# Seven row loads beside the output projection, a weights' place opened inside a stage, and a mixture four steps sooner

## The chip, the cores and the metric

The kernel runs on one core of a Trainium2 chip. A core has five engines with instruction queues of their own: PE (matrix products), DVE (vector work), ACT (scalar functions), POOL (GpSimd) and SP, which here only issues transfers. POOL issues transfers too. Each engine takes its instructions in order and waits on semaphores for the others. Sixteen DMA engines carry all transfers of the core.

The metric is the time of one execution on the device, in microseconds. The kernel before takes 2197.03 us (median of three runs, 2195.69 to 2200.31).

## The reference

One layer of a bidirectional encoder, run on two sets of tokens with the same weights: a long set of 1024 tokens (`A` in the code, the prompt) and a short one of 512 (`B`, the sample), 1024 features each.

```python
h = rms_norm(x, pre_w)
cols = jnp.einsum('bsd,dc->bsc', h, w_in)          # one input projection
m_qk, m_v, m_o, m_z, m_i, m_f, a_qkv, a_z, gate = jnp.split(cols, ...)
y_m = mlstm_mixer(m_qk, m_v, m_o, ...) * silu(m_z)  # branch m: 4 heads x 256, both directions
y_a = dilated_attention(a_qkv, rel_table) * silu(a_z)  # branch a: 3 dilations x 8 heads x 64
p_m, p_a = y_m @ w_pm, y_a @ w_pa
g = sigmoid(gate)                                   # two gates per channel
merged = g[0] * p_m + g[1] * p_a
out = merged @ w_out
return x + rms_norm(out, post_w)
```

The dilated attention computes three groups (dilations 1, 4, 16), each with its own softmax over a window and a bias taken from a table, and then mixes the three outputs per token and head by their softmax maxima and denominators. That mixing is called the mixture here.

## The kernel before

All matrix products are done in two parts of each operand, a high and a low one, as three matmuls (`mm3`, L232): high x high, high x low, low x high. One `mm3` with 512 columns is called a step.

**Order of the work.** The input projection of the long set comes first. Then PE runs one recurrence or attention after the other, and between their pieces it runs steps of a second stream, the `Fill` (L137): the input projection of the short set, then the two branch projections and the output projection of the long set (`outputs`, L2249), then those of the short set (`branches`, L2542, and `final`, L2613). `fill(share)` runs as many steps as the stage's rate says. For PE and SP the program's order is the order on the engine; for DVE, ACT and POOL a planner orders the instructions by a model of their times.

The stretch that matters begins at step 768 of the fill (`SHORT`), where only the last four of the short set's input units are left, which make gates (8 steps each):

- the short set's attention, `N.attend(B, ...)` (L2940), 48 tiles in rounds. In each round PE does one tile's logits (`lg`, two buffers), later its transposes (`pt`) and products (`o`), and 6.25 steps of the fill (4.75 in the last third). DVE adds the bias from a table that SP loads from `erow` and takes the maximum (L1867, L1758), ACT the exponential. Outputs go to `og_b` in memory.
- beside it, in the fill: the four gate units with `begin` alongside (L2315, one of its yields per step), which loads quadrants of the long set's rows and splits the first; then 112 steps of the first branch projection, 64 of the second, and the long set's output projection (L2445), 112 steps counted by `n` (L2528). The latter's finished rows are added to `y_prompt` in memory by accumulating transfers on POOL, held in the list `adds`.
- after the attention, the short set's mixture, `N.combine(B, ...)` (L2950). It loads `og_b` for 128 tokens at a time (L2131, L2138), computes weights (`weigh`, L2078), scales the three parts (`mix`, L2097), adds them (`add`, L2104), and PE transposes the sum (`turn`, L2108, line L2111). Each of its pieces goes to DVE only behind the last eviction issued so far (`self.evicted`). Between its pieces the fill runs `STEPS[4]` = 30 steps in four shares and then `STEPS[5]` = 46 steps in 14.
- the rest of the fill: the short set's projections.

**Buffers and queues that the change touches.**

- Weights are held in places of one high and one low tile (`N.wsplit`). Three exist from the start. Where the short set's gates had their own store buffers (`N.sw`, four of 512 columns), a fourth place is opened at L2931 to L2933, at step 768: the stores still pending from these buffers are issued on SP, and the memory is then taken as a place. A store reads what an ACT instruction (L1059) wrote.
- The last four gates are stored from the residual buffers `xo` (`N.late`, L2939, four in rotation). The same buffers later hold rows of the input for the residual sum of the short set (L2669 to L2672).
- The eight rows of the short set's branch m (`ym_b`, 128 x 512 each) are split into high and low parts by `split_rows` (L2218): ACT L2224, DVE L2225. It goes along with the output projection from n = 86. Rows 0 to 3 go to the places H2 and X0, rows 4 to 7 to K0 and Q1, which hold operands of the output projection until its last quarter. Rows 0, 1 and 2 are loaded at n = 44, 50 and 56 (L2519) into three buffers (`rows_in`: `sraw` and two `ymr`), rows 3 to 7 after the attention (L2943 to L2945) into five more (`ymx`). All eight loads are SP's.
- In the short set's first branch projection (L2555) the transfers left in `adds` go out at every second step (L2566).

Of the kernel before, what the change touches and what calls it, by code (L numbers as in the profile page):

```python
# [22 lines left out]
F32 = mybir.dt.float32  # L23
# [6 lines left out]
P = 128  # L30
D = 1024
KT = D // P
BLK = 512
# [173 lines left out]
class Net:  # L207
# [2002 lines left out]
                    self.fetch(("ym", T.S, min(r // 2, 4)), t[:, :w], T.ym[r, :, b * BLK:b * BLK + w])  # L2210
                yield

    def row_load(self, T, tiles, k):

        t = tiles[k]
        self.fetch(("ym", T.S, k // 2), t, T.ym[k])

# [31 lines left out]
    def outputs(self, T, before):  # L2249
# [20 lines left out]
        def slots(name):  # L2270
            x = four(name, F32R)
            return [(x[:, 0], x[:, 1]), (x[:, 2], x[:, 3])]
# [42 lines left out]
        def begin():  # L2315
            for name, at in (("a0", "K0"), ("b0", "K1"), ("a1", "X0"), ("b1", "Q1")):
                M[name] = four(at)
            for n, (name, row, b) in enumerate((("a0", 0, 0), ("b0", 4, 0))):
                quadrant(name, row, b)
                for _ in range((6, 18)[n]):  # L2320
                    yield
            M["even"] = slots("V0b") + slots("V1b")
            for k in range(4):
                divide(made, ("m", 0, k), M["even"][k], M["a0"][:, k])
                yield
# [119 lines left out]
        def final(weights):  # L2445
# [3 lines left out]
            n = 0  # L2449
            tiles = [(i, t) for i in range(7) for t in range(4)]  # L2450
# [55 lines left out]
            w, p = {}, {}  # L2506
            for s in range(len(tiles) + 1):
                for z in (s - 1, s):
                    if not 0 <= z < len(tiles):
                        continue  # L2510
                    (i, t), kp = tiles[z], s - z
                    if t == 0:
                        w[kp] = [y.rearrange("p (k c) -> p k c", c=S) for y in weights(i == kp == 0)]
                    if kp == 0:
                        p[z] = self.dense()
                    for k in (2 * kp, 2 * kp + 1):
                        give(jobs, n)
                        give(self.adds, n)
                        if n in (44, 50, 56):  # L2519
                            self.row_load(*self.after, (n - 44) // 6)  # L2520
                        hi, lo = made["f", i, k]
                        c = slice(t * P, (t + 1) * P)
                        self.mm3(p[z], (hi[:, c], lo[:, c]), (w[kp][0][:, k % 2], w[kp][1][:, k % 2]), k == 0, k == 3)
                        if k == 3:
                            evict(i, t, p.pop(z))
                        if t == 3 and k % 2:
                            weights.__self__.release()
                        n += 1  # L2528
                        yield
# [12 lines left out]
    def branches(self, T, b, odd, before):  # L2542
# [12 lines left out]
        def proj_m(weights):  # L2555
            m2[:] = [self.place(1 - odd, i, F32) for i in (0, 2)]
            fill = weights.__self__
            gate(1, 0)
            for ct in range(KT):
                wm = weights()  # L2560
                pm = self.dense()
                if ct == 4:
                    assert not self.adds
                    self.more_places(fill, [[z[:, 1024 * i:1024 * (i + 1)] for i in range(2)] for z in map(self.take, ("H0", "H3"))])
                for k in range(KT):
                    if k % 2 and self.adds:  # L2566
                        self.adds.pop(0)[1]()
                    c = slice(k * P, (k + 1) * P)
                    hi, lo = yb[k // 4]
                    self.mm3(pm, (wm[0][:, c], wm[1][:, c]), (hi[:, k % 4], lo[:, k % 4]), k == 0, k == KT - 1)  # L2570
                    if k == 3:
                        gate(*((1, ct + 1) if ct < KT - 1 else (0, 0)))
                    if k == KT - 1:
                        self.evicted = nc.vector.scalar_tensor_tensor(m2[ct // 4][:, ct % 4], gates.pop((1, ct)), 1.0, pm, op0=OP.add, op1=OP.mult)
                    yield
# [103 lines left out]


SHORT = 768
STEPS = (316, 260, 192, (6.25, 4.75), 30, 46)
QUADS = (0, 1, 5, 6, 3, 4, 7)
PRE_A, PRE = 28, 32

# [1 line left out]
def body(tc, a):  # L2687
    N = Net(tc, a)
    nc = tc.nc
    (x1, y1), (x2, y2) = a["runs"]  # L2690
    with ExitStack() as st:
# [13 lines left out]
        with ExitStack() as s1:  # L2705
# [4 lines left out]
            with ExitStack() as sv:  # L2710
# [34 lines left out]
                for i in range(2):  # L2745
                    p = ps.tile([P, BLK], F32, name="d")
# [114 lines left out]
        with ExitStack() as s1:  # L2861
# [13 lines left out]
            fill = Fill(N, units)  # L2875
# [7 lines left out]
            with ExitStack() as s2, tc.issue_after(N.splits[0].ins), tc.issue_after(N.splits[1].ins):  # L2883
                end = N.short_input(N.pool(s2, "turn", 6, "right", PSUM), xt)
# [12 lines left out]
            with ExitStack() as s2:  # L2897
# [30 lines left out]
                        pass  # L2928
                    N.flush(lambda p: True)
                fill.until(SHORT)  # L2930
            N.flush(lambda p: p[3] is not None and p[3][0] is N.sw)  # L2931
            sw = sw_tile()
            N.wsplit.insert(0, [sw[:, 1024 * i:1024 * (i + 1)] for i in range(2)])  # L2933
            fill.ahead, N.side = 4, nc.gpsimd
            N.osb = N.pool(s1, "out", 1, "left")
            N.rows_in = [N.sraw[:, :BLK]] + [N.osb.tile([P, BLK], F32, name=f"ymr{i}") for i in range(2)]
# [3 lines left out]
            N.attend(B, fill, STEPS[3], kept["qkv"], ("lg", "o", "pt"), 7)  # L2940
            end = N.pool(s1, "end", 1, "right")
            N.ps_d.append(N.pool(s1, "ps_e", 2, "left", PSUM))
            N.after[1][3:] = [end.tile([P, BLK], F32, name=f"ymx{i}") for i in range(5)]  # L2943
            for k in range(3, KT):
                N.row_load(*N.after, k)  # L2945
            N.xo_bufs.insert(0, ("late", [end.tile([P, BLK], F32, name=f"xo2{i}") for i in range(2)]))
            with ExitStack() as s2:
                cmb_ps = N.pool(s2, "cmb_ps", 2, "right", PSUM)
# [80 lines left out]
```

## Time and profile before

| | |
|---|---|
| median of three runs | 2197.03 us |
| lowest, highest | 2195.69, 2200.31 us |
| profiled execution | 2199.68 us |
| its span, first to last instruction | 2197.9 us |
| mean granted clock of TensorE | 0.995 |
| DMA, mean over the span | 213 GB/s |

The profile is of one execution. A group's row gives line, engine, operation, tiles and count. A row of the timeline begins with start and duration in us; in brackets stands how long the engine was idle before it and what released it. A row of the waits is: who waited, for whom, total us, times, longest. A row of the windows is: the stretch, its length, then the busy us and instructions of PE, PEld (weight loads), DVE, ACT and POOL, the granted clock (1.00 is full), the mean busy share of the DMA engines, and GB/s. A row of the transfers is: transfer, issuing queue, count, size, median us from issue to landing.

### The profile page before, as it was taken

Reading aid. Unit: us, or ns where it says so; the run is one execution under the profiler, and the core shown is the slowest. Engines: PE = TensorE matmul, PEld = TensorE weight load, DVE = VectorE, ACT = ScalarE, POOL = GpSimd, SP = SyncE. Lnnn points to the kernel's source line nnn. Section 1 sums busy time; section 2 is a strip of 40 time slices with the busy share of each in tenths; the row PEclk is TensorE's granted clock in tenths of the full one; section 3 lists DMA queues with packets and bytes.
Section 4 is the critical chain, followed back from the end, with each engine's and each line's share of the span. In section 5 each row is a group of like instructions: output and inputs, shape, how many; then the busy total and the mean of one; then the engine's idle time right before and its main releaser. Section 6 shows DMA issues by size and latency. Waiting matters only on the chain.

```text
span 2197.9 us, 33826 instructions
## 1 busy us (share of the span) xinstructions
PE 2164.9 (98%) x11530; PEld 1841.9 (84%) x11530; DVE 1543.4 (70%) x3011; ACT 1084.2 (49%) x2248; POOL 800.9 (36%) x1053
## 2 busy tenths in 40 slices
PE   9999999999999999999999999999999999999798
PEld 8988888888777888888888889998788878888686
DVE  8766676768887987547888775574668837675773
ACT  7322344444444444446777666666755534435321
POOL 1000444333233875325776650011045522331531
PEclk9999999999999999999999999999999999999999
DMA  5642687955456554367646558886668778876972
GB/s 214 190 140 71 209 274 248 302 201 198 164 184 218 201 201 157 134 204 266 194 164 231 169 168 265 240 240 194 199 234 276 248 250 306 289 238 224 256 280 96
DMA packets 233944, 469.05 MB, mean 213 GB/s; under 512 B 38282, under 2 KB 120394, under 8 KB 233643
## 3 DMA queue, kind: packets, MB, share of 16 engines
q1 hardware_dynamic: 199304, 343.00, 48.0%
q0 software_dynamic: 30864, 111.29, 15.8%
q10 hardware_dynamic: 3602, 12.59, 1.4%
q8 instruction: 91, 1.49, 0.3%
q14 instruction: 83, 0.67, 0.1%
HBM read 314.56 MB, written 156.43 MB: 214 GB/s over the span
## 4 chain that ended last, share of the span: by engine, by line
PE 59%; DMA 4%; issue 3%; DVE 2%; POOL 1%; ACT 1%; SPq 0%; DVEq 0%; POOLq 0%; ACTq 0%
PE dense L235 11%; PE dense L236 11%; PE dense L237 11%; PE d L237 4%; PE d L235 4%; PE d L236 4%; PE lg L1848 2%; PE pt L1878 1%; PE o L1921 1%; PE num L235 1%; PE num L236 1%; PE num L237 1%; PE num L1541 1%; DMA pre<-phlb 1%; DMA ymx<-ym_b 1%
## 5 line engine op out<-in xcount | busy, mean ns | idle before, releaser
L235 PE MATMUL dense<-H,wh 128*128 128x512 f32 x680 | 276.5, 407 | 1.3 <-DVE H L2499 1.1
L237 PE MATMUL dense<-H,wl 128*128 128x512 f32 x680 | 267.0, 393 | 0.0
L236 PE MATMUL dense<-H,wh 128*128 128x512 f32 x640 | 251.6, 393 | 0.0
L237 PE MATMUL d<-Hh,phla 128*128 128x512 f32 x608 | 237.6, 391 | 2.7 <-DVE phla L767 2.7
L235 PE MATMUL d<-Hh,phla 128*128 128x512 f32 x608 | 236.7, 389 | 0.0
L236 PE MATMUL d<-Hl,phla 128*128 128x512 f32 x608 | 236.6, 389 | 0.0
L237 PE MATMUL d<-Hh,phlb 128*128 128x512 f32 x456 | 178.0, 390 | 0.3 <-DVE phlb L767 0.3
L235 PE MATMUL d<-Hh,phlb 128*128 128x512 f32 x456 | 177.6, 389 | 0.3 <-ACT phlb L766 0.3
L236 PE MATMUL d<-Hl,phlb 128*128 128x512 f32 x456 | 177.4, 389 | 0.0
L237 PEld LDWEIGHTS dense<-H,wl 128*128 128x128 f32 x680 | 128.1, 188 | 28.8
L785 POOL TENSOR_TENSOR psum_w<-pw_raw 128x512 f32<-128x512 f32 x38 | 54.3, 1429 | 247.3 <-DMA pw_raw<-w_in 141.1
L235 PEld LDWEIGHTS dense<-H,wh 128*128 128x128 f32 x680 | 128.5, 189 | 18.8 <-issue 2.4
L305 DVE TENSOR_TENSOR wl<-wraw,wh 128x1024 fp32r<-128x1024 f32 (+1 forms) x96 | 120.5, 1257 | 33.6 <-ACT wh L299 33.6
L1867 DVE CUSTOM_DVE_ANT_0 ls<-lg,bias 128x256 f32<-128x256 f32 (+2 forms) x240 | 78.8, 350 | 92.7 <-PE lg L1848 59.9
L237 PEld LDWEIGHTS d<-Hh,phla 128*128 128x128 f32 x608 | 114.1, 188 | 30.0 <-DVE phla L767 6.7
L236 PEld LDWEIGHTS d<-Hl,phla 128*128 128x128 f32 x608 | 114.1, 188 | 24.0
L235 PEld LDWEIGHTS d<-Hh,phla 128*128 128x128 f32 x608 | 114.1, 188 | 23.3
L236 PEld LDWEIGHTS dense<-H,wh 128*128 128x128 f32 x640 | 121.2, 189 | 13.8
L299 ACT ACTIVATE wh<-wraw 128x1024 fp32r<-128x1024 f32 (+1 forms) x99 | 101.8, 1031 | 50.6 <-PE dense L236 27.3
L1871 ACT ACTIVATE ls<-ls,nm 128x256 f32<-128x256 f32 (+1 forms) x192 | 87.4, 457 | 78.6 <-DVE nm L1869 60.3
L235 PE MATMUL d<-v,Hh 128*128 128x484 f32 (+1 forms) x336 | 121.4, 361 | 0.1
L237 PE MATMUL d<-v,Hl 128*128 128x484 f32 (+1 forms) x336 | 120.6, 359 | 0.4 <-DVE Hl L475 0.4
(737 smaller groups left out, 5977.4 us busy)
## 6 DMA issues: line engine op xcount, KB each, us to landing
pw_raw<-w_in SPq DMA_DIRECT2D x76, 512.0 KB, 4.0
wraw<-w_in SPq DMA_DIRECT2D x63, 512.0 KB, 4.5
pw_raw<-w_q SPq DMA_DIRECT2D x44, 512.0 KB, 6.2
pre<-phlb SPq DMA_DIRECT2D x32, 512.0 KB, 4.7
aqk_a<-pwk SPq DMA_DIRECT2D x32, 512.0 KB, 6.9
pre<-phlb SPq DMA_DIRECT2D x16, 1024.0 KB, 8.0
wh<-pre POOLq DMA_DIRECT2D x26, 512.0 KB, 5.3
wl<-pre POOLq DMA_DIRECT2D x26, 512.0 KB, 6.3
```

What stands on the lines that cost most here:

```text
L235: nc.tensor.matmul(out, lh, rh, start=start, stop=False, **kw)
L236: nc.tensor.matmul(out, lh, rl, start=False, stop=False, **kw)
L237: nc.tensor.matmul(out, ll, rh, start=False, stop=stop, **kw)
L299: high = nc.scalar.activation(hi[:, :n], raw[:, :n], AF.Copy)
L305: low = (self.lows or nc.vector).tensor_sub(lo[:, :n], raw[:, :n], hi[:, :n].bitcast(F32))
L785: self.nc.gpsimd.tensor_add(s[:, 0], ws[1][:, 0], ws[1][:, 1])
L1541: nc.tensor.matmul(pn, hi[:, j], z[:, c1], start=j == 0 and z is v[0], stop=False)
L1848: nc.tensor.matmul(lg[:, hh], q[hh][:, qs], z.rearrange("p (n j) -> p n j", j=P)[:, pair], start=z is k[hh], stop=z is not k[hh])
L1867: nc.vector.tensor_tensor_reduce(out=ls[rows, hh], in0=ts["lg"][hh][rows, of], in1=bt[rows, hh, by], scale=1.0, scalar=NEG, op0=OP.add, op ...
L1871: self.held = self.held[-3:] + [nc.scalar.activation(ls[:, hh], ls[:, hh], AF.Exp, bias=nm[:, hh:hh + 1], accum_out=ot[:, 128 + hh:129 + hh])]
L1878: nc.tensor.transpose(pp[:, hh * nk + x], ts["ls"][:, hh, x * P:(x + 1) * P], self.ident)
L1921: nc.tensor.matmul(of(hh, 0, P), vh(kt[x], hh), pt[:, hh * len(kt) + x], start=x == 0, stop=x == len(kt) - 1)
```

## The change

Four things are changed from step 768 on.

- **The fourth weights' place** is no longer opened at step 768 but by `open_place`, which `begin` calls 14 of its yields later. The pending stores of the `sw` buffers are flushed there, or before it by the ticks of the attention's rounds; and the place is put in by `more_places` (L2537), which sets it ahead of the places that are still in use.
- **Rows 0 to 6** of the short set are loaded beside the output projection, at n = 20, 26, 32, 38, 44, 50 and 56: rows 0 to 2 into `rows_in` as before, rows 3 to 6 into the four `xo` buffers, taken in rotation (`self.late()`). Only row 7 is loaded after the attention, into one `ymx` buffer.
- **The accumulating transfers** left in `adds` go out at every fourth step instead of every second.
- **The mixture's stages** have 26 and 50 steps of the fill instead of 30 and 46.

```diff
-    def row_load(self, T, tiles, k):
+    def row_load(self, T, tiles, k, own=None):
 
+        if own is not None and own is not False:
+            tiles.append(own)
         t = tiles[k]
         self.fetch(("ym", T.S, k // 2), t, T.ym[k])
...
-                for _ in range((6, 18)[n]):
+                for _ in range((6, 8)[n]):
                     yield
+            self.open_place()
+            for _ in range(10):
+                yield
...
-                        if n in (44, 50, 56):
-                            self.row_load(*self.after, (n - 44) // 6)
+                        if n % 6 == 2 and 20 <= n < 62:
+                            self.row_load(*self.after, n // 6 - 3, n >= 38 and self.late())
...
-                    if k % 2 and self.adds:
+                    if k % 4 == 3 and self.adds:
                         self.adds.pop(0)[1]()
...
-STEPS = (316, 260, 192, (6.25, 4.75), 30, 46)
+STEPS = (316, 260, 192, (6.25, 4.75), 26, 50)
...
-            N.flush(lambda p: p[3] is not None and p[3][0] is N.sw)
-            sw = sw_tile()
-            N.wsplit.insert(0, [sw[:, 1024 * i:1024 * (i + 1)] for i in range(2)])
+
+            def open_place():
+                N.flush(lambda p: p[3] is not None and p[3][0] is N.sw)
+                sw = sw_tile()
+                N.more_places(fill, [[sw[:, 1024 * i:1024 * (i + 1)] for i in range(2)]])
+            N.open_place = open_place
...
-            N.after[1][3:] = [end.tile([P, BLK], F32, name=f"ymx{i}") for i in range(5)]
-            for k in range(3, KT):
-                N.row_load(*N.after, k)
+            N.row_load(*N.after, KT - 1, end.tile([P, BLK], F32, name="ymx"))
```

## The prediction

> **What bounds the kernel now.** I began with the page: which engine is full, and in which slices it isn't.
>
> ```profile
> PE 2164.9 (98%) x11530; PEld 1841.9 (84%) x11530; DVE 1543.4 (70%) x3011; ACT 1084.2 (49%) x2248; POOL 800.9 (36%) x1053
> PE   9999999999999999999999999999999999999798
> ```
>
> TensorE is busy for 98% of the span, and no edit here takes a matmul away. So only its holes can be won. Slice 38 (about 2033 to 2088 us) is a hole; the last slice is the program's tail. The waits of PE name the causes, and windows cut at the holes size them.
>
> ```profile
> PE tp L2111 <- DVE wd L2090: 9.6, 1, 9.6
> ...
> PE lg L1848 <- DVE ot L1867: 2.3, 1, 2.3
> PE dense L235 <- DVE H L2499: 1.4, 2, 1.1
> PE pt L1878 <- ACT ls L1871: 1.4, 1, 1.4
> ```
> ```profile
> 1792.00:1801.25 9.25, 5.55 (x17) 4.34 (x17) 5.40 (x19) 3.97 (x14) 0.00 (x0) 0.63 0.82 269
> 2076.90:2091.20 14.30, 4.72 (x13) 3.90 (x14) 11.93 (x28) 2.34 (x3) 10.22 (x17) 0.65 1.06 302
> ...
> 2090.78 0.63 PE L237 MATMUL dense<-H,sw 128*128 128x512 f32 x1
> ...
> 2091.94 0.39 PE L235 MATMUL dense<-K,sw 128*128 128x512 f32 x1
> ...
> 2092.63 0.40 PE L235 MATMUL dense<-K,sw 128*128 128x512 f32 x1
> ```
>
> Two places, then, with granted clocks of 0.63 and 0.65: after an idle spell TensorE goes on at half clock for some us. A step (three matmuls) is 0.69 us at full clock (2091.94 to 2092.63).
>
> *Hole 1* holds 17 matmuls: 8 short ones and 9 of 512 columns. At full clock I reckon 2.8 us for them (9 x 0.23 = 2.1, and some 0.7 for the short ones). Lost: 9.25 - 2.8 = **6.4 us**, of which 2.3 + 1.4 idle and 2.7 slow clock.
>
> *Hole 2* holds 13: 4 transposes and 9 matmuls, 2.1 + 0.4 = 2.5. Lost: 14.3 - 2.5 = **11.8 us**, of which 9.6 idle and 2.2 slow clock. The 1.4 us before L235 lie just ahead of it. All holes together: 6.4 + 11.8 + 1.4 = **19.6 us**.
>
> Why hole 1? The queue of SP and the DVE in order of time:
>
> ```profile
> 1778.76 5.04 SPq L251 DMA_DIRECT2D gt_b<-sw  x2
> ...
> 1782.86 0.60 ACT L1059 ACTIVATE sw<-dense 128x512 f32<-128x512 f32 x1 [4.12 <-PE dense L237]
> ...
> 1783.89 1.15 SPq L276 DMA_DIRECT2D bias<-erow  x2
> ...
> SPq L251 <- ACT sw L1059: 6.7, 2, 4.3
> ...
> DMA to landing us min/median/max: 7.6/7.9/8.1
> ...
> 1787.24 0.64 PE L1848 MATMUL lg<-V0a,Q 128*128 128x256 f32 x4
> ...
> 1792.35 0.42 DVE L1867 CUSTOM_DVE_ANT_0 ls<-lg,bias 128x256 f32<-128x256 f32 x1 [5.17 <-DMA bias<-erow]
> ```
>
> The flush at L2931 makes SP store the last sw gates; the second store waits 4.3 us for the ACT that fills the buffer (1782.86). Behind it, in program order, stands the bias table of the short set's first attention tile. It is asked for at 1783.89, lands some 8 us later, DVE starts the first softmax at 1792.35, and the third lg product wants one of the two lg buffers back at 1792.
>
> Why hole 2? Followed back from the transpose:
>
> ```profile
> 2045.69 3.00 SPq L276 DMA_DIRECT2D ymx<-ym_b  x5
> ...
> DMA to landing us min/median/max: 12.0/13.6/14.5
> ...
> 2050.96 0.68 DVE L2499 TENSOR_TENSOR H<-H,dense 128x512 f32<-128x512 f32 x1
> ...
> 2052.65 0.39 PE L237 MATMUL dense<-wh,Q 128*128 128x512 f32 x1
> ...
> 2057.67 0.63 ACT L2224 ACTIVATE H<-ymx 128x512 fp32r<-128x512 f32 x1 [7.86 <-DMA ymx<-ym_b]
> 2058.34 0.69 DVE L2225 TENSOR_TENSOR X<-ymx,H 128x512 fp32r<-128x512 f32 x1 [6.70 <-ACT H L2224]
> ...
> 2061.28 0.89 POOL L2475 DMA_DIRECT2D y_prompt<-H  x1 [11.10 <-DVE H L2498]
> ...
> 2079.17 0.17 DVE L2083 TENSOR_TENSOR cw<-V1a 128x8 f32<-128x8 f32 x1 [2.02 <-DMA V1a<-og_b]
> ...
> 2085.64 0.69 DVE L2106 TENSOR_TENSOR X<-X 128x512 f32<-128x512 f32 x1
> 2086.48 1.09 PE L2111 MATMUL tp<-ident,X 128*128 128x128 f32 x4 [9.58 <-DVE wd L2090]
> ...
> 2051.64:2086.33 34.69, 23.84 (x103) 18.69 (x101) 25.22 (x52) 12.08 (x24) 18.18 (x26) 0.92 1.04 260
> ```
>
> Five rows of the short set are asked for together at 2045.69 and need 12 us or more. ACT and DVE take their instructions in order, so the first row's split holds ACT for 7.9 us and DVE for 6.7, and through DVE the POOL, which issues the mixture's loads, for 11.1. DVE then has 25.2 us of work before the mixture's last add (2085.64), for which the transpose waits; the row's "wd L2090" is only a neighbour in that queue.
>
> **The change, part by part.** Sums go against the profiled execution: 2199.68 us (span 2197.9, 1.8 around it), which is 2.65 above the median of the runs, 2197.03.
>
> *Gate buffers become a weights' place at step 14.* The flush at L2931 goes, so the table's load is SP's next instruction once the earlier stores are out: at 1779.1 (1778.76 and one store of 0.3) or soon after, instead of 1783.89. With the same 7.9 us it lands by 1787, when the second lg product runs; the wait of 5.17 us goes and with it hole 1. Price of the edit: three weight places instead of four for 14 steps (14 x 0.69 = 9.7 us and two attention rounds). Four gate units of 8 steps run here, and the place is back for the load that the third asks for, 16 steps ahead of its use; a weight load needs a place, not more. I take **-6.4 us**. Bounds: at most that; 0 if the table still lands at 1792, which the eight K loads on POOL in the same us could do.
>
> *Seven rows beside the output projection.* Rows 0 to 6 are asked for at n = 20, 26 ... 56, four of them into the xo buffers, which nobody uses between the last gates' stores and the residual loads of the last projection. Nothing is added: eight loads before, eight after; four (1 MB) move ahead and three somewhat. Those three, for n = 44 to 56, show where:
>
> ```profile
> 2002.17 2.01 SPq L276 DMA_DIRECT2D bias<-erow  x3
> 2011.99 1.22 SPq L276 DMA_DIRECT2D V1a<-av_b  x2
> ...
> 2015.29 0.56 SPq L276 DMA_DIRECT2D sraw<-ym_b  x1
> 2015.95 1.15 SPq L276 DMA_DIRECT2D ymr<-ym_b  x2
> ```
>
> SP runs them at 2015 to 2017, so all seven lie between about 2002 and 2017 and have landed by about 2031 even with the 14.5 us of the slowest ymx row. Rows 4 to 7 are split into K and Q places, which PE reads until 2052.65; their splits can begin there, and before 2064 (when the next product begins) there is time for four of 0.6 us on ACT and 0.7 on DVE. Row 7, still asked for after the attention, lands at 2057.7 at the latest (the 12.0 of the first ymx row); it is the last split of eight, so by then little stands behind it. The 6.7 us of DVE and the 1.4 us of PE ahead of hole 2 go: **-1.4 us**.
>
> *What is late next at hole 2.* The transpose's place in PE's order moves too. The stages change from 30 + 46 steps to 26 + 50: it stood 30 + 5 x 46/14 = 46.4 steps behind the attention, and now stands 26 + 5 x 50/14 = 43.9 behind it, 2.6 steps or 1.8 us sooner. PE will be there at 2076.9 - 1.4 - 1.8 = 2073.7. DVE, free at 2051.6 and never idle, has 25.2 us of work: 2076.9. One of its five row splits (row 3, into X, 0.7) isn't tied to PE and can go ahead: 2076.2. So **2.5 us of idling stay**. Bounds: 0, since the mixture's own instructions come 4 steps (2.7 us) sooner in DVE's order and can leave behind them these three, which now stand between them and aren't needed:
>
> ```profile
> 2083.04 1.41 DVE L2474 SCALAR_TENSOR_TENSOR H<-H,ss,postw 128x512 f32<-128x512 f32 x2
> 2084.97 0.68 DVE L2574 SCALAR_TENSOR_TENSOR V0b<-gab,dense 128x512 f32<-128x512 f32 x1
> ...
> 2079.55 1.22 DVE L305 TENSOR_TENSOR wl<-wraw,wh 128x1024 fp32r<-128x1024 f32 x1 [0.21 <-ACT wh L299]
> ```
>
> On the other side 11.4 (9.6 + 1.8), if the loads of og and w_pm, not the DVE, set the time. I take 2.5, since the DVE row (25.2 of 34.7) is the nearest. A wait of 2.3 us halved the clock in hole 1, so I add the 2.2 us that the slow clock cost in hole 2: 4.7 stay of 11.8, **-7.1 us**.
>
> [...]
>
> *y_prompt's stores at half the rate* (k % 4 == 3): as many stores on POOL, later ones; the og loads of the mixture come ahead of some of them. POOL has 10.2 us of work in the 14.3 of hole 2, so they are hidden, and nothing waits for them but the H0 and H3 places four units later. Cost 0; without that cover, one store's 0.9 us on POOL.
>
> **Sum.** -6.4 - 1.4 - 7.1 = -14.9: 2199.68 - 14.9 = 2184.8 in the profiled execution, 2.65 less for the median: **2182 us**.
>
> **Rivals.**
>
> *The table comes sooner, but the transpose waits on.* Its chain held a late load (V1a, 2.02 us of wait at 2079.17). If these loads, issued by POOL among the stores, set the time, hole 2 keeps its 11.8: -6.4 - 1.4 gives 2189. For it: the DMA share of 1.06 in hole 2. Against it: POOL issued them late because it waited 11.1 us for DVE.
>
> *The clock holds in the short wait.* One wait of 2.5 us may leave the clock alone where two, of 2.3 and 1.4, halved it in hole 1: as forecast, with 2.5 us left at hole 2 instead of 4.7: 2199.68 - 17.1 - 2.65 = 2180. [...]
>
> *It doesn't do what it says.* The table lands no sooner, and a later row takes the place of the first ymx row at DVE's head: 2197. For it: DMA engines are the fullest resource in both stretches (0.82 and 1.04 to 1.06). Against it: both queues wait for an order, not for bandwidth.
>
> *Slower: the mixture's first read blocks the evictions.* The mixture's weights (L2083) need the last og part:
>
> ```profile
> 2055.65 0.32 SPq L276 DMA_DIRECT2D V0a<-og_b  x1
> ...
> V0a<-og_b SPq DMA_DIRECT2D x3, 264.0 KB, 11.3
> ```
>
> It lands at about 2067. Four steps sooner, L2083 may stand in DVE's order ahead of the projection's last evictions. Then DVE stops until 2067, PE runs out of accumulators (four, of 2.7 us each; I estimate at about 2058) and idles some 9 us, and the 20 us or so that DVE then still has to do put the transpose at about 2088, 1.7 later and 2.6 steps earlier in the order: 3.5 us, and a second half clock of 2.5. That is +6, and 2203 where the table gains nothing. It decides as soon as L2083 comes more than about 3 us before the last L2499. Against it: the tables' wait is a separate place, and with its 6.4 us this comes out level.
>
> **How the numbers follow.** Forecast 0.47 (2182); the clock holds 0.10 (2180); only the table 0.18 (2189); only the rows 0.06 (about 2188); no change 0.10; slower 0.09. The floor is all holes gone: 2199.68 - 19.6 - 2.65 = 2177.4, less 1.3 for the spread of the runs (2195.69 to 2197.03): 2176. Upwards the range takes in the two half cases with 5 us of doubt: 2194. About 0.2 (within 0.2%, and slower) stay outside. A measurement of this kernel tells about 0.2% (4.4 us) from no change; faster by more is 0.80, within it 0.11, slower 0.09.
>
> **What the changed profile would show.** The table's bias load on SP before 1780, DVE's first L1867 before 1789, no wait of PE at lg L1848, and a clock of 1.00 in 1790 to 1800: hole 1 right. No wait of ACT L2224 for a row of over 2 us, POOL's 11.1 us gone: rows right. The wait before tp L2111 between 0 and 5 us, released by DVE L2106: residue right. Wrong if PE shows new waits at lg L1747 in 1980 to 2045 (rows ahead of the attention's loads on SP), at dense for a weight load near 1800 to 1830 (three places too few), or at a later tp.

## The result, and the profile after

The changed kernel takes 2192.91 us (median of 12 runs, 2189.77 to 2194.35) against 2197.99 for the kernel before (12 runs beside it): ratio 0.9974, interval 0.9965 to 0.9983. The medians differ by 5.1 us; the ratio is worked out from all runs, and the medians alone would give 0.9977. A second measurement, among the experiments, gave 2190.43 against 2197.70: 0.9971, 0.9961 to 0.9981. The forecast was 2182, a gain of 14.9.

The profiled execution took 2191.3 us (span 2189.5), 1.6 below its median where that of before was above: its difference of 8.4 us is larger than that of the medians. Its line numbers: those up to L2111 are as before; L2224 and L2225 are now L2226 and L2227; from L2469 to L2574 they are 5 higher. Experiments that add lines shift them by a few more.

PE's waits in the changed kernel (who waited, for whom, total, times, longest), and windows at its holes and in the place of the old first hole:

```profile
PE tp L2111 <- DVE cw L2085: 5.3, 1, 5.3
...
PE dense L235 <- DMA wh<-pre: 2.7, 1, 2.7
...
PE tp L2111 <- DVE Q L2106: 0.8, 1, 0.8
```
```profile
1784.00:1801.25 17.25, 17.25 (x87) 14.60 (x86) 9.37 (x31) 9.28 (x26) 4.40 (x9) 1.00 0.79 283
2048.08:2050.79 2.71, 0.00 (x0) 0.03 (x1) 2.49 (x4) 2.09 (x5) 0.88 (x3) 1.00 1.05 370
2070.29:2080.00 9.71, 4.37 (x13) 3.63 (x14) 4.87 (x11) 2.33 (x3) 3.99 (x7) 0.66 1.02 355
```

The first hole is gone: PE is busy for all of 1784 to 1801.25, at a clock of 1.00, and there is no wait at lg L1848. The second is smaller, 5.3 us of waiting instead of 9.6, and there is a **new wait** of 2.7 us for the last weights of the long set's output projection.

The timeline of the changed kernel shows why. SP and DVE at the first hole, POOL's stores and last loads of those weights, the split rows on ACT, and DVE ahead of the transpose:

```profile
1776.69 0.97 SPq L276 DMA_DIRECT2D bias<-erow  x2
...
1782.17 0.99 SPq L276 DMA_DIRECT2D bias<-erow  x2
1783.83 1.30 SPq L251 DMA_DIRECT2D gt_b<-sw  x2
1783.85 0.42 DVE L1867 CUSTOM_DVE_ANT_0 ls<-lg,bias 128x256 f32<-128x256 f32 x1 [3.92 <-PE lg L1848]
...
2031.16 0.94 POOL L2480 DMA_DIRECT2D y_prompt<-H  x1
2031.78 1.22 POOL L2480 DMA_DIRECT2D y_prompt<-K  x1
2032.41 1.48 POOL L2480 DMA_DIRECT2D y_prompt<-H  x1
...
2033.51 1.48 POOL L832 DMA_DIRECT2D wh<-pre  x1
2034.07 1.85 POOL L2480 DMA_DIRECT2D y_prompt<-K  x1
2034.63 1.83 POOL L832 DMA_DIRECT2D wl<-pre  x1
...
2039.14 0.55 POOL L832 DMA_DIRECT2D wh<-pre  x1 [1.62 <-PE dense L237]
...
2050.45 0.63 ACT L2226 ACTIVATE K<-ymx 128x512 fp32r<-128x512 f32 x1 [0.62 <-DMA ymx<-ym_b]
...
2069.30 0.69 DVE L2106 TENSOR_TENSOR X<-X 128x512 f32<-128x512 f32 x1
2073.24 0.17 DVE L2084 TENSOR_TENSOR cw<-cw,V1a 128x8 f32<-128x8 f32 x1 [3.25 <-DMA V1a<-og_b]
2073.66 1.23 DVE L305 TENSOR_TENSOR sw<-wraw,sw 128x1024 fp32r<-128x1024 f32 x1 [0.25 <-ACT sw L299]
2074.80 0.69 DVE L2106 TENSOR_TENSOR X<-X 128x512 f32<-128x512 f32 x1
2075.63 1.09 PE L2111 MATMUL tp<-ident,X 128*128 128x128 f32 x4 [5.35 <-DVE cw L2085]
```

The first table is asked for at 1776.69 instead of 1783.89 (the row at 1782.17 is the next pair of loads), the gates' stores now stand behind the tables, and DVE's first softmax starts at 1783.85, not 1792.35. The rows do what was meant: ACT waits 0.62 us for the last one, not 7.86. But between the two adds of the first 128 tokens (2069.30, 2074.80) DVE waits 3.25 us for a part of the NEXT 128 tokens and then splits a weight; and of one weights' place the low half is asked for at 2034.63 and the high half only at 2039.14, 3.4 us after the attention's last product (2035.76). In the kernel before, with the last product at 2042.20, POOL had two stores ahead of that load and asked for it 0.7 us after the product:

```profile
2037.51 0.94 POOL L2475 DMA_DIRECT2D y_prompt<-H  x1 [1.10 <-DVE H L2474]
2038.17 1.19 POOL L2475 DMA_DIRECT2D y_prompt<-K  x1
...
2042.92 1.13 POOL L832 DMA_DIRECT2D wh<-pre  x1
```

### The profile page after: what moved, and what is told of

Its sections match the earlier page's. It is cut to its first block, busy times and chain, and to the rows that moved or that the text cites. A ratio compares the mean times of both kernels' runs of the same rounds, so it can differ in the third digit from the quotient of the medians.

```text
span 2189.5 us, 33817 instructions
## 1 busy us (share of the span) xinstructions
PE 2161.3 (99%) x11530; PEld 1840.2 (84%) x11530; DVE 1544.6 (71%) x3011; ACT 1085.3 (50%) x2248; POOL 800.8 (37%) x1053
## 3 DMA queue, kind: packets, MB, share of 16 engines
q0 software_dynamic: 30864, 111.29, 15.8%
## 4 chain that ended last, share of the span: by engine, by line
PE 58%; DMA 4%; DVE 4%; issue 3%; POOL 2%; ACT 1%; SPq 0%; DVEq 0%; POOLq 0%; ACTq 0%
PE dense L235 10%; PE dense L236 10%; PE dense L237 10%; PE d L237 4%; PE d L236 4%; PE d L235 4%; PE lg L1848 2%; PE pt L1878 1%; DMA wraw<-w_pm 1%; PE o L1921 1%; PE num L235 1%; PE num L237 1%; PE num L236 1%; DMA pre<-phlb 1%; PE a L1248 1%
## 5 line engine op out<-in xcount | busy, mean ns | idle before, releaser
L235 PE MATMUL dense<-H,wh 128*128 128x512 f32 x704 | 285.7, 406 | 0.4 <-DVE H L2374 0.4
L237 PE MATMUL dense<-H,wl 128*128 128x512 f32 x704 | 276.0, 392 | 0.0
L236 PE MATMUL dense<-H,wh 128*128 128x512 f32 x672 | 263.4, 392 | 0.0
L235 PEld LDWEIGHTS dense<-H,wh 128*128 128x128 f32 x704 | 132.9, 189 | 18.3 <-issue 0.9
L236 PEld LDWEIGHTS dense<-H,wh 128*128 128x128 f32 x672 | 126.8, 189 | 14.7
L299 ACT ACTIVATE wh<-wraw 128x1024 fp32r<-128x1024 f32 (+1 forms) x101 | 104.0, 1032 | 58.4 <-PE dense L236 41.9
```

Source lines behind the costliest of these rows:

```text
L235: nc.tensor.matmul(out, lh, rh, start=start, stop=False, **kw)
L236: nc.tensor.matmul(out, lh, rl, start=False, stop=False, **kw)
L237: nc.tensor.matmul(out, ll, rh, start=False, stop=stop, **kw)
L299: high = nc.scalar.activation(hi[:, :n], raw[:, :n], AF.Copy)
```

## The experiments

The ratio is to the kernel before, run beside each experiment, with its 95% interval. The marks come from the profile of one execution each: the wait of a dense product for `wh` at the end of the long set's projection, the waits ahead of the mixture's four transposes (waits under 0.5 us left out), and the time from the start of the attention's last product o to the start of the first and of the fourth transpose. Of e4 only the time is used.

| kernel | ratio | wait for wh | waits, transposes 1 to 4 | last o to 1st, 4th |
|---|---|---|---|---|
| before | 1 | 0 | 9.6, 0, 0, 0 | 44.3, 68.5 |
| changed | 0.9974 [0.9965, 0.9983] | 2.7 | 5.3, 0.8, 0, 0 | 39.9, 66.4 |
| a2_after, the same | 0.9971 [0.9961, 0.9981] | 3.1 | 6.2, 0.8, 0, 0 | 43.9, 70.4 |
| e1_table | 0.9978 [0.9969, 0.9987] | 0.9 | 9.4, 0, 0, 0 | 44.4, 68.9 |
| e2_no_table | 1.0004 [0.9995, 1.0012] | 2.9 | 5.2, 0.8, 0, 0 | 41.3, 68.0 |
| e3_rows | 0.9997 [0.9988, 1.0006] | 2.8 | 5.6, 0, 0, 0 | 43.0, 66.7 |
| e4_old_steps | 0.9968 [0.9957, 0.9979] | | | |
| e5_parts_sp | 0.9952 [0.9940, 0.9965] | 2.3 | 5.2, 0, 0, 0 | 40.8, 66.3 |
| e6_weights_sp | 0.9969 [0.9958, 0.9981] | 0 | 10.6, 0, 0, 0 | 42.1, 67.5 |
| e8_old_adds | 0.9965 [0.9952, 0.9977] | 3.0 | 5.7, 0.8, 0, 0 | 41.9, 68.0 |
| e9_raw_sp | 0.9951 [0.9938, 0.9963] | 0 | 8.6, 0, 0, 0 | 40.5, 66.4 |
| e10_all_sp | 0.9971 [0.9960, 0.9982] | 0 | 12.2, 0, 0, 0 | 43.8, 69.5 |
| e11_order | 0.9999 [0.9991, 1.0008] | 2.6 | 0, 14.3, 0, 0 | 35.5, 75.3 |
| e12_order_raw_sp | 0.9963 [0.9951, 0.9976] | 0 | 2.3, 7.3, 0, 0 | 34.1, 68.9 |
| e13_order_no_rows | 0.9971 [0.9960, 0.9983] | 0 | 5.8, 3.5, 0, 0 | 41.2, 70.5 |
| e14_order_parts | 0.9972 [0.9962, 0.9981] | 3.4 | 0, 0.8, 6.0, 0 | 37.7, 71.6 |
| e15_order_parts_weights | 0.9971 [0.9962, 0.9981] | 0 | 6.1, 0.8, 2.2, 0 | 37.7, 67.3 |
| e16_no_stores | 0.9939 [0.9927, 0.9952] | 0 | 5.1, 0, 0, 0 | 36.6, 62.8 |
| e17_late_stores | 0.9998 [0.9990, 1.0007] | 0 | 3.4, 0, 10.1, 0 | 35.0, 72.0 |
| e18_late_order | 1.0032 [1.0020, 1.0045] | 0 | 0, 6.7, 9.0, 1.1 | 31.4, 75.8 |

One caution for the table: the same program gave 39.9 and 43.9 us to the first transpose in two executions, so a difference of 4 us between two single profiles says nothing by itself.

### Which part of the change gives the gain

e1_table is the kernel before with the hunks on `begin` and `open_place` alone; e2_no_table is the changed kernel without them; e3_rows is the kernel before with the hunks on `row_load`, n and `ymx` alone; e4_old_steps and e8_old_adds each take one line back:

```diff
-STEPS = (316, 260, 192, (6.25, 4.75), 26, 50)
+STEPS = (316, 260, 192, (6.25, 4.75), 30, 46)
```
```diff
-                    if k % 4 == 3 and self.adds:
+                    if k % 2 and self.adds:
```

> The kernel before with the weights' place opened at step 14 alone (no rows moved, stages 30 + 46, stores at the old rate). Theory (the first hole is won whole by this part, and the rest of the change gives its own gain back through two new waits): 6.4 us faster, ratio 0.9971, the hole at 1792 gone, the transpose's wait still 9 to 10 us. Rival (three weight places for 14 steps cost something that the whole change hides): 3 us faster or less, ratio 0.9986, with a wait of a dense product for weights between 1795 and 1830.

> The changed kernel with the weights' place opened at step 768 as before; rows, stores and stages stay changed. Theory: 1.3 us slower to 2 us faster than before (ratio 0.999 to 1.0006): the rows and the mixture's earlier place win about 2.3 us in the profile after the attention and no more. Rival (the rows do win what was forecast, 8.5 us, and something in the table's part takes it back): ratio 0.996 to 0.997.

> The kernel before with the seven row loads beside the projection alone; the mixture stays in its old place (30 + 46) and the stores at the old rate. Theory (the transpose waits for a load that POOL issues behind stores, and for what stands ahead of it in the DVE's order, not for the rows): POOL's wait of 11.1 us is gone, the transpose still waits 5 us or more, ratio 0.998 to 1.0. Rival (the reasoning on record: the rows set the DVE's order of time): the transpose waits 4 us or less and 5 to 7 us are won, ratio 0.997. The wait of 2.7 us for the last weights of the long set's output projection comes with the rows if the queues are the cause, and is absent here if the halved rate of stores or the earlier mixture is.

> The changed kernel with the mixture's stages back at 30 + 46 steps. If the four steps help only by moving the loads that POOL issues, the transpose's wait stays about 5 us and stands 1.8 us later: 0 to 2 us slower than the whole change (ratio 0.9974 to 0.9983). If they move the transpose ahead of what it waits for, and no more, its wait shrinks by 1.8 us and the time is that of the whole change, 0.9974. If they cost time by placing loads in front of weights, it is faster: 0.996.

> The changed kernel with the stores to y_prompt in the short set's first projection at every second step again. On record this part costs nothing. If the stores on POOL hold the mixture's loads, the old rate makes the waits at the second and third transposes grow (0.8 us now) and the time 1 to 2 us longer than the changed kernel's, ratio 0.998; if not, 0.9974 as the changed kernel.

The table's part alone gives 0.9978, which is nearly the whole gain; everything else together gives 1.0004. No dense product waits for weights beside the new three places. The rows alone give 0.9997, though they do their work on the spot; PE's waits in e3_rows are:

```profile
PE tp L2111 <- DVE cw L2085: 5.6, 1, 5.6
...
PE dense L235 <- ACT K L2226: 2.8, 1, 2.8
PE lg L1848 <- DVE ot L1867: 2.6, 1, 2.6
```

The transpose's wait falls from 9.6 to 5.6, and 2.8 us at the weights are new (the same place as in the changed kernel; the releaser named is a neighbour). So most of the new wait (0.9 in e1, 2.8 here) comes with the rows, not with the stores' rate or the steps. e4 and e8 lie within the changed kernel's interval: neither the four steps nor the rate of the stores can be told from nothing.

### Theory one: late loads on POOL

The loads that DVE and PE wait for are put on SP, which issues seven transfers between 2035 and 2080 us in the changed kernel, where POOL issues 31. e5_parts_sp:

```diff
-                        self.fetch(("og", T.S), cs[t % 2][:, g], T.og[t * P:(t + 1) * P, g], self.side)
+                        self.fetch(("og", T.S), cs[t % 2][:, g], T.og[t * P:(t + 1) * P, g])
```

(and az likewise). e6_weights_sp, in `load_pre`, and e9_raw_sp, in `load_w`:

```diff
+            if u in (26, 27):
+                self.nc.sync.dma_start(x[:, :1024].bitcast(F32), self.pre[u, z])
+            else:
+                self.loaded = self.side.dma_start(x[:, :1024].bitcast(F32), self.pre[u, z])
...
+        if self.late and self.on_sp:
+            self.on_sp -= 1
+            self.nc.sync.dma_start(raw[:, :kt * cols], src)
+            return raw, kt * cols
```

e10_all_sp has all three.

> The changed kernel with the mixture's later loads (og and az) on SP instead of POOL. In the changed kernel DVE waits 3.25 us for the last og part of the second 128 tokens, and the transpose 5.3. If that load alone keeps the transpose waiting, the wait falls to about 2 us, the half clock goes, and the time is 5 us below the changed kernel's (ratio to before 0.995). If the split of w_pm's next weights (landed at 2072.5, standing in DVE's order ahead of the last add) holds it just as well, DVE's wait for the part is gone but the transpose still waits 4 us or more: ratio 0.9965 to 0.9975. If the DVE's amount of work set it, as on record, the wait would be 2.5 us at most from the start.

> The changed kernel with the last two pairs of weights of the long set's output projection loaded by SP instead of POOL. If the wait of 2.7 us at 2048 comes from POOL (the load is issued only 3.4 us after the attention's end, because an issue there stands behind the landing of an accumulating store), SP issues it 4 us sooner, the wait is gone and 2.7 us are won: ratio to before 0.9962. If the DMA engines are full there (0.88 to 1.05) and the bytes themselves set it, a wait of 1.5 us or more stays: 0.997.

> The changed kernel with the eight raw loads of w_pm on SP instead of POOL. If the late raw weights hold the DVE's last add as well as the og part does, this alone leaves DVE waiting for the part (still on POOL, but with four loads fewer ahead of it): the transpose waits 2 to 4 us, ratio 0.996. If they are nothing but bystanders, the wait stays 5 us, 0.9974. If SP's loads then stand ahead of the attention's last stores, the first og parts come late: a DVE wait at L2083 of over 2 us, and 0.998.

> The changed kernel with all three on SP: og and az, w_pm's raw weights, and the last two pairs of the output projection. If POOL's queue, with its stores, is what took the change's gain back, both waits go: 2.7 us, and 5.3 us to 1 or less with the 2.3 us of half clock, 9 to 10 us below the changed kernel: ratio to before 0.993. If the DMA engines' bandwidth is the limit, the loads only change places and the ratio stays at 0.997.

The theory falls in this form. With the weights on SP their wait is gone, and the transpose's takes its place; PE's waits in e6_weights_sp:

```profile
PE tp L2114 <- DVE wd L2091: 10.6, 1, 10.6
```

PE comes sooner and waits longer: the 2.7 us lay in the shadow of the transpose. With the og parts on SP the transpose still waits 5.2, with w_pm on SP 8.6, with all three 12.2. In none of the four does the fourth transpose come sooner after the attention than the changed kernel's 66.4 us by more than 0.2. e5 and e9 have the best times of the whole kernels here, 0.9952 and 0.9951, but beside the changed kernel's two profiles (66.4 and 70.4) theirs show no more than a good execution, and they weren't timed beside it: whether they are better is not settled.

### Theory two: DVE's order

e11_order ties the second 128 tokens' weigh, and every weight split issued later, behind the first tokens' last add. e12 is this with e9's edit, e13 this with e1's (no rows, old steps):

```diff
+            added[:] = [nc.vector.tensor_add(y[:, 0], y[:, 0], y[:, g])]
+            if not slow and t == 0:
+                self.first_sum = added[:]
...
+                    if i == 0 and t == 1 and not slow:
+                        st.enter_context(self.tc.issue_after(added[0].ins))
...
-                for x in (*self.held, *self.scans):
+                for x in (*self.held, *self.scans, *self.first_sum):
```

> The changed kernel with one rule more for the DVE's order: the second 128 tokens' weigh and every weight split issued from then on stand behind the first 128 tokens' last add. No load moves. Theory (the transpose waits because DVE, in its order, waits 3.25 us for a part of the NEXT tokens and does three splits of 1.2 us in front of that add): the last add comes at about 2070 instead of 2074.8, PE's wait falls from 5.3 to 1 us or less, the half clock of some 7 us goes (2 to 3 us more), and the time is 7 us below the changed kernel's: ratio to before 0.994 to 0.995. Rival (the loads themselves, behind stores on POOL, set it, whatever the order): the wait stays at 4 us or more and the ratio at 0.997. Other rival: the splits that now come later make a product wait for weights after the transpose, and the gain is given back there.

> The same rule, and w_pm's raw loads on SP, which alone took the 2.7 us wait for the long set's last weights away but let the transpose's wait grow from 5.3 to 8.6. If that 2.7 us lay in the shadow of the transpose's wait, it can be won only now, where the transpose no longer waits: 2 us below the run with the rule alone, ratio to before 0.993 to 0.994. If DVE's work is the limit again as soon as PE arrives 2.7 us sooner, the wait goes over to the transpose and the ratio is that of the rule alone.

> The kernel before with the weights' place opened at step 14 and the same rule for DVE, without the moved rows and with the old stages (30 + 46). If the rows were the cause of the second hole, as on record, DVE's wait of 6.7 us for the first late row stays, the transpose still waits 6 us or more, and the ratio is 0.997. If the order alone is the cause, the wait falls to 3 us or less and the ratio is 0.994 to 0.995 without the rows.

In e11 the first transpose waits for nothing, and the whole gain is given back at the second one. PE's wait, and the timeline of POOL and DVE ahead of it:

```profile
PE tp L2114 <- DVE wd L2089: 14.3, 1, 14.3
```
```profile
2075.41 2.12 POOL L833 DMA_DIRECT2D H<-pre  x4 [4.19 <-DMA y_prompt<-H]
...
2078.04 0.54 POOL L277 DMA_DIRECT2D V1a<-og_b  x1
...
2086.29 0.17 DVE L2085 TENSOR_TENSOR cw<-cw,V1a 128x8 f32<-128x8 f32 x1 [6.47 <-DMA V1a<-og_b]
```

POOL waits 4.19 us for the landing of a store to y_prompt, since the next weights go into the memory that it reads; behind that wait stands the og part for which DVE then waits 6.47. DVE's order is as meant here; the load behind the stores is late all the same. e12, with w_pm's raw weights on SP, has 2.3 and 7.3 us of wait at the first two transposes and a ratio of 0.9963, where 0.993 to 0.994 was expected: the gain goes to the second transpose again. e13, without the moved rows, keeps a wait of 7.2 us of DVE for the first late row and 5.8 us at the first transpose; its 0.9971 can't be told from e1's 0.9978. So the order alone wins nothing, with the rows moved or not.

### Theory three: the stores

e14 joins e5's edit (og and az on SP) with the order, now for all four groups of tokens (the conditions `t == 0` and `t == 1` above give way to any t); e15 has e6's edit too; a2_after is the changed kernel again. e16_no_stores takes the accumulating stores away, e17_late_stores keeps all sixteen back, and e18_late_order is e17 with the order of e14:

```diff
-                    self.adds.append((n + 5 + 4 * h, lambda y=y, c=c: nc.gpsimd.dma_start(T.y[r0:r0 + P, c], y, accum_op=OP.add)))
+                    pass
```
```diff
-                        give(self.adds, n)
+                        if n < 70:
+                            give(self.adds, n)
...
-                    if k % 4 == 3 and self.adds:
-                        self.adds.pop(0)[1]()
+                    if ct > 1 and self.adds:
+                        with self.tc.issue_after(self.mixing.ins):
+                            self.adds.pop(0)[1]()
```

(`mixing` is the last og load of the second tokens; `ct > 1` begins with the third unit of the short set's first projection.)

> The changed kernel once more, beside the others. Its first measurement gave 0.9974, while three variants that hardly differ in their profile from the short set's attention on gave 0.9951 to 0.9965. If its size is as first measured, 0.997 to 0.998 again. If the difference lies in the first 1780 us, whose small waits differ from execution to execution, it comes out lower here, 0.995 to 0.9965.

> The changed kernel with og and az on SP, and in DVE's order each 128 tokens' weigh and the weight splits issued later behind the last add of the tokens before. The order alone took the first transpose's wait away and gave 14.3 us of wait back at the second, whose og part POOL issued behind four weight loads that waited for stores. Theory (both are needed: the loads away from POOL's stores, and the adds ahead of what is not yet due): the first two transposes wait 3 us or less together, and the time is 6 us below the changed kernel's, ratio to before 0.992 to 0.993. Rival (bandwidth or DVE's amount of work is the limit): the wait turns up at a later transpose or at a product for w_pm's weights, 6 us or more, ratio 0.995 or above.

> The same, with the last two pairs of the long set's output weights on SP too. If the 2.7 us at 2048 no longer lies in the shadow of the transpose, 2 us less than the run without: 0.991 to 0.992. If PE then arrives before DVE is done, the transpose takes the wait over and the ratio is the same.

> The changed kernel without the accumulating stores to y_prompt: that part of the output is left out, all work on TensorE, DVE and ACT stays. Theory (POOL's stores delay the loads behind them): the wait of 2.7 us for the last weights is 0.5 or less, the first transpose waits 2 us or less, no half clock, 8 us or more below the changed kernel. Rival (DVE's 31 us of work between the attention and the transpose are the limit, as on record): the transpose still waits 4 us or more, and what goes at the weights comes back there.

> The changed kernel with the last sixteen accumulating stores to y_prompt kept back: on POOL they stand behind the loads of the second 128 tokens' og parts. Nothing is left out. Without any such store the changed kernel was 7 us faster (0.9939 against 0.9971), its weights came in time and the transpose still waited 5.1 us. Theory (it is the stores' place on POOL that costs, not their bytes): the wait for the last weights is gone, the transpose waits about 5 us, ratio 0.9935 to 0.995. Rival (the stores cost wherever they stand): they now delay the loads of the third 128 tokens and of w_pm's weights, and 4 us or more of waits turn up after the first transpose, ratio 0.997.

> The same, with DVE's order as in the run with og and az on SP: each 128 tokens' weigh and the later weight splits behind the last add of the tokens before. If the 5.1 us that stay without stores are DVE's, whose queue is nearly full of work not yet due, the first transpose waits 2 us or less and nothing turns up later: 3 us below the run with late stores alone, 0.992 to 0.9935. If the work put behind the add is due before the second transpose, its wait grows by as much: no gain over late stores alone.

e14 and e15 have the first two waits down to 0.8 us, or the weights' wait gone, and pay at the third transpose (6.0) or the first (6.1): with 0.9972 and 0.9971 neither can be told from the changed kernel.

Only e16 shortens the stretch, to 62.8 us, and the kernel by 14.8 us (2182.87 against 2197.70), some 7 more than the changed kernel beside it (2190.43). The windows from the last o to the fourth transpose show what changed. Before:

```profile
2042.20:2110.68 68.48, 57.48 (x258) 46.42 (x258) 53.27 (x108) 18.25 (x36) 34.97 (x53) 0.93 1.01 302
```

The changed kernel, with a second window that ends at the first transpose:

```profile
2035.76:2102.14 66.38, 57.52 (x257) 46.39 (x257) 52.73 (x108) 18.64 (x36) 33.98 (x53) 0.95 1.01 299
...
2035.76:2075.63 39.87, 31.81 (x149) 25.52 (x149) 31.40 (x61) 14.40 (x30) 23.07 (x35) 0.97 1.06 293
```

e16_no_stores, with windows from its last weights and from the last o (2034.74) to the first transpose, and POOL's last load of the long set's weights:

```profile
2045.00:2071.35 26.35, 21.26 (x94) 17.17 (x93) 22.70 (x48) 10.98 (x23) 12.51 (x21) 0.99 0.54 178
2034.74:2097.50 62.76, 57.67 (x257) 46.98 (x257) 53.11 (x110) 19.07 (x37) 22.21 (x38) 0.95 0.71 248
...
2034.74:2071.35 36.61, 31.52 (x149) 25.60 (x149) 32.21 (x66) 14.40 (x30) 15.14 (x26) 0.99 0.67 231
...
2035.04 0.53 POOL L832 DMA_DIRECT2D wh<-pre  x1
```

e17_late_stores:

```profile
2031.16:2103.20 72.04, 58.51 (x258) 47.47 (x258) 52.30 (x108) 18.01 (x35) 36.66 (x54) 0.91 0.88 254
```

The last three figures of a row are clock, DMA share and GB/s (the share adds up the times of all packets; these can overlap, so it can pass 1). Before and after the change the DMA engines are **full for all of the 66 to 68 us** (1.01), and PE, DVE and POOL do the same work. Without the stores the share falls to 0.71, the weights are asked for 0.3 us after the last o instead of 3.4, and 5.1 us stay at the first transpose. DVE sets these, though not by its amount of work alone: from the last o to the transpose it works 32.2 us and idles 4.4, 1.9 of them for an og part. With the stores put later, the first transpose comes 5 us sooner than the changed kernel's (35.0 against 39.9), the third waits 10.1 us, the fourth comes at 72.0, and nothing is won. e18, with DVE's order on top, has the first transpose 31.4 us after the last o and waits of 6.7 and 9.0 us at the next two; its 1.0032 is slower than the kernel before. So the stores' work can't be moved off the path by these edits, only along it. Whether what costs is the time that they take on the DMA engines or the time that loads stand behind them on POOL is not separated: in e17 the share is only 0.88 and the stretch is longer.

## Why the prediction was wrong, step by step

- **Hole 1, -6.4 us: right.** The wait at lg L1848, the half clock and SP's late table are gone, and from the first lg to the last o it is 252.7 us (1783.08 to 2035.76) instead of 259.5 (1782.66 to 2042.20). e1 alone gives 4.8 us by its ratio, 6.3 by the medians. The table is asked for at 1776.69, sooner than the 1779.1 worked out. Three places for 14 steps cost nothing, as said.
- **The rows, -1.4 us: the mechanism was right, the sum lacked a term.** ACT, DVE and POOL no longer wait for rows. But POOL's order changed with them: four stores go out ahead of the last weights' load (2031.16 to 2034.07) where two did (2037.51 and 2038.17 in the kernel before), it is asked for 3.4 us after the last o instead of 0.7, and PE waits for it for 2.7 us. The prediction named a wait for weights as a sign of error only near 1800 to 1830.
- **Hole 2, -7.1 us: this is the step that failed.** "So 2.5 us of idling stay" rests on "DVE, free at 2051.6 and never idle", with the upper bound kept for "the loads of og and w_pm, not the DVE". DVE's amount of work was about right, but it wasn't "never idle". The forecast puts 34.0 us between the last o and the first transpose (2042.2 to 2076.2), all of them work. In the changed kernel it is 39.9 us, of which DVE works 31.4 and idles 8.5; without the stores (e16) it is 36.6, with 32.2 of work and 4.4 idle. The longest idle spells are 3.25 us for an og part (1.89 in e16) and 1.70 for the split of a weight (1.03). The prediction's own rows held such a wait, 2.02 us for V1a, and the sum put it at nothing, since POOL had waited for DVE before it issued that load. PE came as forecast but for the new wait: 34.5 us after the last o, against 31.5 and 2.7. So 5.3 us of idling stayed in one execution and 6.2 in the other. In the window 2070.29 to 2080.00 the 13 matmuls take 4.37 us instead of 2.5, so the slow clock costs 1.9 (2.2 was said), and 0.8 comes at the second transpose: 8.0 of the 11.8 stay, where 4.7 were forecast.
- **The sum again with these terms:** -6.4 - 1.4 + 2.7 - 11.8 + 8.0 = -8.9, which is 2190.8 for the profiled execution; it took 2191.3. These are two single executions: a2_after's profiled one took 2193.8, its stretch 4.0 us longer, and by the medians the change gives 5.1 us, not 8.4. The median of 2192.9 does lie below the upper end of the range, 2194, but by the 5 us of doubt added there, not by the reasoning.
- **The rival that came nearest** is "the table comes sooner, but the transpose waits on" (2189). It named the loads that POOL issues among the stores. The stores are borne out (e16), POOL's queue alone isn't: with og, w_pm's weights or all of these loads on SP the transpose still waits 5.2 to 12.2 us. The argument against it, that POOL issued the loads late because it waited for DVE, held for the kernel before only. And the row that spoke for it stood in the prediction: a DMA share of 1.06 in hole 2. It was put aside with "both queues wait for an order, not for bandwidth". That holds at hole 1, where the share was 0.82 and the new order won the wait; at hole 2 each new order only moved it.
- **The stores' rate, 0:** e8 can't be told from the changed kernel. **The clock** held at the new 2.7 us and fell to half at the 5.3: the length of a wait alone doesn't decide it, since 2.28 us halved it in e5_parts_sp (last section). **The slower rival** didn't come: DVE reads the og parts at 2058.64, behind an eviction and without a wait.

## What to carry to other kernels

Before an edit is credited with a wait, take the window over the whole stretch in which the same transfers run: if the DMA engines are full in it, an earlier load can make another one late, and the wait turns up at the next consumer, as it did here (a share of 1.01 before and after; 2.7 us at the weights were new). Judge such edits by the end of the stretch (here the fourth transpose), not by the wait that disappeared, and size the gain by an experiment that takes the suspected load away altogether.

## What the hardware showed

**The accumulating stores are dearer than their bytes.** The page's rows of POOL's queue over the whole span (packets, MB, share of the 16 DMA engines), first of the changed kernel, then of e16_no_stores:

```profile
q0 software_dynamic: 30864, 111.29, 15.8%
```
```profile
q0 software_dynamic: 28560, 107.10, 14.5%
```

The sixteen stores, 4.2 MB, take some 29 us of all sixteen engines (15.8% of 2189.5 us less 14.5% of 2183.2). That is some 140 GB/s, as an estimate from these rows, where the rest of the queue gets 338 (107.10 MB in 316.6 us). Packet by packet, the changed kernel's trace has 0.20 us for a store's 2 KB and 0.18 us for 4 KB of a load on the same queue between 2020 and 2100 us. The windows from 2050 to 2065 us, at nearly the same place of the program, show it too, with some loads moved between them (changed kernel, then e16_no_stores):

```profile
2050.00:2065.00 15.00, 14.21 (x62) 11.71 (x63) 13.13 (x27) 7.21 (x15) 8.51 (x12) 1.00 1.10 263
```
```profile
2050.00:2065.00 15.00, 15.00 (x68) 12.28 (x67) 11.84 (x27) 6.08 (x12) 6.25 (x10) 1.00 0.33 110
```

All sixteen stores are issued by POOL in every run that has them; whether another queue would serve them no run here shows.

**In these traces the clock was halved after idle time of PE within one window of 3.41 us; the length of a wait did not decide it.** The changed kernel goes on at a clock of 1.00 after 2.71 us of idling, e5_parts_sp at 0.76 after 2.28:

```profile
2050.79:2057.00 6.21, 6.21 (x27) 5.15 (x28) 5.20 (x9) 3.31 (x8) 1.33 (x3) 1.00 1.11 254
```
```profile
2048.28:2055.00 6.72, 6.72 (x23) 5.42 (x24) 4.99 (x9) 3.46 (x9) 0.55 (x1) 0.76 1.10 269
```

The trace's records of the granted clock give the half-speed spells in whole steps of 3.41 us: one after the 2.28 us of e5 and the 2.9 of e2, two (6.83 us) after the changed kernel's 5.3, three (10.24 us) after the 9.6 of before, four after the 14.3 of e11. So a grid of windows of that length can be laid on the trace, in step with these records, and PE's idle time read in each (19 profiled executions, all in the table but e4's, 17 to 2150 us; ends of matmuls are modelled). Of 11787 windows at full speed, the 34 with 1.95 us of idle time or more are each followed by one at half speed, and none of those with 1.91 or less is. In the traces of before and of the changed kernel alone, 1241 windows at full speed, it is the three with 2.34, 3.10 and 3.41 us, and none with 1.41 or less. A window at half speed is followed by full speed if PE idles for 0.57 us or less in it (34 of 69), and by another at half speed from 0.75 us on. The 2.71 us of the changed kernel fall into two windows, 1.41 and 1.30; of e5's 2.28 us, 2.13 lie in one. How far these bounds hold elsewhere no run here shows.
